# Sample's sums spread over the picking, the first row sums of the second table begun inside it, and the sample's norm moved into it

## The chip, the cores and the metric

The kernel runs on one core of a Trainium2 chip. The metric is device time in microseconds (us), the median over runs; lower is better. The engines are named as in the profile: PE is TensorE (PEld its weight loads), DVE is VectorE, ACT is ScalarE, POOL is GpSimd, SP is SyncE, whose queue issues the plain DMAs; POOL issues the indirect ones (gathers).

## The reference, cut to what matters

One layer of a decoder step: a projection, an RWKV group and a sparse-attention group, an output projection, a norm, and then the part that is changed here, an expert mixer ("PEER") with its norm:

```python
D_MODEL = 2048; SEQ = 256            # prompt tokens
DEC_BATCH, DEC_SEQ = 8, 4            # 32 sample tokens
P_HEADS = 8; P_TOPK = 16; N_EXPERTS = 128 * 128
def peer_ffn(x, wq, subkeys, u_tab, v_tab):
    ...            # per token: 8 heads x 16 = 128 experts, with gates
    h = gelu(einsum('cd,chkd->chk', xb, u_tab[eb]))
    return einsum('chk,chkd->cd', gb * h, v_tab[eb])
f = peer_ffn(x, ...)
x = layer_norm(DEEPNORM_ALPHA * x + f, ln2_g, ln2_b)
```

So each token has 128 gated experts, each a row of 2048 columns in a first table u (for h) and in a second table v (for the sum).

## The kernel before, in words

The mixer is done in two ways at once. For the 256 prompt tokens most columns go the dense way: TensorE multiplies whole rows of the tables, and each token's experts are picked out of the result. The remaining columns go by gathers: for one of a token's 128 experts, POOL issues an indirect DMA that brings 128 rows, one for each token of a half of the prompt (128 partitions x 896 columns of the first table, 128 x 640 of the second), and VectorE makes a dot product of them (the first table, a column of `HD`) or adds them, times their gate, to a running sum (the second table, `fP`). The 32 sample tokens have gathers only: 32 sums `j`, each over four experts of each token at once, where two gathers bring two half rows of v (128 x 1024) and four matmuls with the weights `ws` add them to one bank `fs` of PSUM.

The stages that matter here come in this order:

- The dense loop over the first table (L1886), with prompt gathers of u beside it. Of 256 gathers and dots per partition, 64 are left when it ends (`left`).
- The picking (`M_("weigh")`, L1970 on): 68 steps `s_` of a loop written out in Python, four prompt tokens each. For step u of 64: a one-hot `oo` on VectorE (L1918), its transposes on TensorE (L1922) and their copy `oT` on ScalarE (L1924), products `px` on TensorE (L1930), four masked sums into `E` on VectorE (L1941), the gelu on ScalarE (L1945), the gate into `TB` on VectorE (L1949, `gated`), the one-hot scaled by it on ScalarE or VectorE (L1955, L1957), and `put`: four matmuls `pa` (L1963) and a copy into `AW` (L1964). The stages of u run in steps u to u + 4. Steps 0 to 27 also hold the 64 left dots (L1803). Steps 28 to 59 fetch the sample's sums, steps 30 to 61 add them (L1982). At step 46 the sample's residual and norm weights are loaded, at step 50 the first 128 rows of v (`rows_load(0)`).
- After the loop: both gate tables are transposed into `GE`, the sample's sum gets its residual and its norm (L2027, `norm_quarters`), and sixteen DMAs write it out (L2031).
- The loop over the second table (`M_('V')`, L2085): 128 blocks `k` of 128 rows x 1408 columns. For each block ScalarE makes the high half `vh` (L2077) and VectorE the low half `vl` (L2078) of the loaded `v_`, TensorE does 18 matmuls; for every other block ScalarE makes `ah` (L2074) and VectorE `al` (L2075) from `AW`. Beside it run the 256 prompt gathers of v (`rq`, eight buffers) and their row sums on VectorE (L2058).
- `fin`: the prompt's norm and output.

The order: instructions of the picking that `pin` wraps keep the order in which the code is written, on their engine. The others are placed by a scheduler, which sorts by estimated ready times; ScalarE's casts in the loop over the second table are such. The gathers into the five buffers `rows` of 128 x 1024 (`NRW` = 5, a ring: the dots of the first table and the sample's fetches use the same five) are issued by POOL in order, and each waits for the last reader of the buffer that it fills.

Of the kernel before, what the change touches and what calls it, by code (L numbers as in the profile page):

```python
# [42 lines left out]
NRQ = 8  # L43
# [109 lines left out]
def hybrid_decode_step(ctx: ExitStack, tc: tile.TileContext, a, outs, dbg=None):  # L153
# [19 lines left out]
    def banks(**tags):  # L173

        fewer_banks(0)
        more_banks(**tags)
# [152 lines left out]
    row = 0  # L329
# [126 lines left out]
    def gather(dst, rows_, ix):  # L456
        gp.indirect_dma_start(out=dst, out_offset=None, in_=rows_, in_offset=bass.IndirectOffsetOnAxis(ap=ix, axis=0))  # L457
# [986 lines left out]
    def norm_quarters(pool, x_, g_, b_, tag):  # L1444

        st, mv, rr, sq_ = pool([P, 6], "sst"), pool([P, 2], "smv"), pool([P, 1], "srr"), pool([P, 1], "ssq")
        ve.bn_stats(out=st, in_=x_)
        ve.bn_aggr(out=mv, in_=st)
        ve.tensor_tensor(sq_, mv[:, 0:1], mv[:, 0:1], OP.mult)
        ve.tensor_tensor(mv[:, 1:2], mv[:, 1:2], sq_, OP.add)  # L1450
        pb = bank(tag)
        pe.matmul(pb[:, :2], C0("avg4"), mv, start=True, stop=True)
        ve.tensor_copy(mv, pb[:, :2])
        ve.tensor_tensor(sq_, mv[:, 0:1], mv[:, 0:1], OP.mult)
        ve.tensor_tensor(mv[:, 1:2], mv[:, 1:2], sq_, OP.subtract)
        norm_row(pool, mv, rr)
        sc.activation(x_, x_, AF.Identity, bias=mv[:, 0:1], scale=rr)
        ve.tensor_tensor(x_, x_, g_, OP.mult)
        ve.tensor_tensor(x_, x_, b_, OP.add)
# [309 lines left out]

    M_("wq")  # L1770
    banks(pj=2, pb=6)
    up = Pool("up", "left")
    HD = [up([P, P], f"hd{t}") for t in range(2)]
    TV = [up([P, 8, 16], f"TV{t}") for t in range(2)]
    up([P, 1024], "rows", bufs=NRW)
    xa_ = up([P, 2 * UG], "x1a")
    X1a = [xa_[:, UG * t:UG * t + UG] for t in range(2)]
# [19 lines left out]
    def dot(n=1, upto=2 * P, keep=False, ahead=NRW):  # L1797

        for i in range(got[1], min(got[1] + n, upto)):
            t, s_ = dots[i]  # L1800
            fetch(min(i + ahead, upto))
            r_, h_ = rows_.pop(i), HD[t][:, s_:s_ + 1]
            i_ = ve.scalar_tensor_tensor(r_, r_, 1.0, X1a[t], op0=OP.mult, op1=OP.mult, accum_out=h_)  # L1803
            if keep:
                tc.keep_in_program_order(i_)
            got[1] = i + 1

    def table(t):

        pb = bank("pb")  # L1810
        for q, (op_, v_) in enumerate(((OP.logical_shift_right, 7), (OP.bitwise_and, 127))):
            ii = up([P, P], "ii", I32)
            iff = ii.bitcast(F32)
            ve.tensor_scalar(ii, GI[t], v_, None, op0=op_)
            ve.tensor_copy(iff, ii)
            pe.transpose(pb[:, 128 * q:128 * q + 128], iff, ident)
        pe.transpose(pb[:, 256:384], GE[t], ident)
        pe.transpose(pb[:, 384:], HD[t], ident)
        sc.copy(TB[:, :, P * t:P * t + P], pb.rearrange("p (a b) -> p a b", a=4))
# [151 lines left out]
    ve.tensor_tensor(ws, C0("sum4")[:, None, :32].to_broadcast([P, 32, 32]), GE[2][:, :, None].to_broadcast([P, 32, 32]), OP.mult)  # L1971
    fs, sr = bank("fs"), {}

    def smp_fetch(j):

        for q in range(2):
            sr[j, q] = up([P, 1024], "rows", bufs=NRW)
            gather(sr[j, q], vh2, ig[q][:, j:j + 1])

    def smp_add(j):  # L1980
        for c in range(4):
            pin(pe.matmul(fs[32 * c:32 * c + 32, :], ws[:, j, :], sr[j, c // 2][:, 512 * (c % 2):512 * (c % 2) + 512],  # L1982
                          start=(j == 0), stop=(j == 31)))
# [5 lines left out]
        raw[k] = (vp if k % 3 else vr)([P, FD], "v_", bufs=2 if k % 3 else 1)  # L1989
        return sy.dma_start(raw[k], vtab[P * k:P * k + P, :FD])  # L1990

    left = 2 * P - got[1]
    for s_ in range(68):
        if s_ == 30:
            table(1)
        oT = pick(s_) if s_ < 64 else None
        if 3 <= s_ < 66 and s_ % 2:
            gated(s_ // 2 - 1)
        if s_ >= 4:
            put(s_ - 4)  # L2000
        if 0 <= s_ - 3 < 64:
            scaled(s_ - 3)
        if oT is not None:
            picked(s_, oT)
        if 0 <= s_ - 1 < 64:
            product_of(s_ - 1)
        if s_ < 28:
            dot(-(-left * (s_ + 1) // 28) + 2 * P - left - got[1], keep=True)
        elif s_ < 60:
            smp_fetch(s_ - 28)  # L2010
        if 30 <= s_ < 62:
            smp_add(s_ - 30)
        if s_ == 46:
            bs_, gs_, x_ = (xa_[:, 512 * n:512 * n + 512] for n in range(3))
            for q in range(4):
                r_, c_ = slice(32 * q, 32 * q + 32), slice(512 * q, 512 * q + 512)
                sy.dma_start(x_[r_, :], X1D[NPR:NT, c_])
                for t_, nm in ((gs_, "ln2_g"), (bs_, "ln2_b")):
                    sy.dma_start(t_[r_, :], bass.AP(tensor=a[nm].tensor, offset=a[nm].offset + 512 * q, ap=[[0, 32], [1, 512]]))
        if s_ == 50:  # L2020
            rows_load(0)
    pb = bank("pb")
    for t in range(2):
        pe.transpose(pb[:, 128 * t:128 * t + 128], TB[:, 2, P * t:P * t + P], ident)
        sc.copy(GE[t], pb[:, 128 * t:128 * t + 128])

    ve.scalar_tensor_tensor(x_, x_, ALPHA, fs, op0=OP.mult, op1=OP.add)  # L2027
    norm_quarters(x4p, x_, gs_, bs_, "pb")
    for q in range(4):
        for i in range(4):  # L2030
            sy.dma_start(outs[1][:, i, 512 * q:512 * q + 512], x_[32 * q + 8 * i:32 * q + 8 * i + 8, :])  # L2031
    x4p.close()
    up.close()
    banks(pj=2, pb=6)
# [1 line left out]
    vp = Pool("vp", "left")  # L2036
    vp([P, FD], "v_", bufs=2)
    vp([P, FD], "vh", F32R, bufs=2)
    fP = [vp([P, VG], f"fP{t}") for t in range(2)]
    vp([P, VG], "rq", bufs=NRQ)  # L2040
    queue = [(t, s_) for t in range(2) for s_ in range(P)]
    ahead, here = 0, {}

    def row_fetch(n):

# [4 lines left out]
            gather(here[ahead], a["peer_v_g"], GI[t][:, s_:s_ + 1])  # L2050
            ahead += 1

    def row_add(i):

        t, s_ = queue[i]
        r_, w_ = here.pop(i), GE[t][:, s_:s_ + 1]
        if s_:
            ve.scalar_tensor_tensor(fP[t], r_, w_, fP[t], op0=OP.mult, op1=OP.add)  # L2058
        else:
            ve.tensor_scalar(fP[t], r_, w_, None, op0=OP.mult)  # L2060


    acc = [bank() for _ in range(6)]
    done = 0
    rows_load(1)
    rows_load(2)
    row_fetch(NRQ)
    for k in range(P):
        v_ = raw.pop(k)
        vh, vl = vp([P, FD], "vh", F32R, bufs=2), vp([P, FD], "vl", F32R, bufs=2)  # L2070
        if k % 2 == 0:
            a2 = [vp([P, NPR, 2], nm, F32R, bufs=2) for nm in ("ah", "al")]
            aw_ = AW[:, k // 64, :, k % 64:k % 64 + 2]
            sc.copy(a2[0], aw_)  # L2074
            ve.tensor_tensor(a2[1], aw_, a2[0].bitcast(F32), OP.subtract)  # L2075
        ah, al = (t_[:, :, k % 2] for t_ in a2)
        sc.copy(vh, v_)  # L2077
        lo_ = ve.tensor_tensor(vl, v_, vh.bitcast(F32), OP.subtract)  # L2078
        if k + 3 < P:
            ld_ = rows_load(k + 3)  # L2080
        for t in range(2):
            for wi, xi in ((ah, vh), (ah, vl), (al, vh)):
                for q in range(3):
                    n_ = min(512, FD - 512 * q)
                    pe.matmul(acc[3 * t + q][:, :n_], wi[:, P * t:P * t + P], xi[:, 512 * q:512 * q + n_],  # L2085
                              start=(k == 0 and wi is ah and xi is vh), stop=(k == P - 1 and wi is al))
        while done < min(len(queue), len(queue) * (k + 1) // (P - 2)):
            with tc.issue_after(lo_.ins):
                row_add(done)
            done += 1  # L2090
            row_fetch(done + NRQ)
        if k == 63:
            g2_, b2_, *xo = (AW[:, 0, 32 * n:32 * n + 32, :].rearrange("p a b -> p (a b)") for n in range(4))
        if 66 <= k < 114 and k % 6 == 0:
            with tc.issue_after(ld_.ins):
                n_ = (k - 66) // 6
                c_ = slice(1024 * (n_ % 2), 1024 * (n_ % 2) + 1024)
                if n_ < 4:
# [72 lines left out]
```

## Time and profile before

| | us |
|---|---|
| median of 3 runs (lowest, highest) | 2499.38 (2495.72, 2507.77) |
| the profiled execution, and its span | 2498.71, 2496.9 |
| TensorE busy in the span | 2246.1 (90%) |
| VectorE busy | 1851.9 (74%) |
| ScalarE busy | 927.4 (37%) |
| POOL busy | 1373.4 (55%) |

The span is the time from the first instruction to the last in the profiled execution. A row such as `PE pb L2085` names engine, tile written and source line; a tile's name is followed by the tiles that it was made from (`out<-in`). In rows of groups stand busy time, mean ns of one, and then the engine's idle time just before them and what ended it. "PEclk" is the clock that TensorE was granted, 1.00 being full speed. A wait is written `engine tile line <- releaser: us, times, mean`.

### The profile page before, as it was taken

To read this page: it belongs to the slowest core of one execution; us is meant where nothing else is said; L and a number is where in the kernel's file an instruction comes from. 1 tells how busy PE (TensorE), PEld (TensorE's weight loads), DVE (VectorE), ACT (ScalarE), POOL (GpSimd) and SP (SyncE) were. 2 spreads that over 40 slices of the span, in tenths; PEclk is the share of its full clock that TensorE was granted. 3 is DMA by queue.
4 is the path that set the end of the run, shared out by engine and by line. 5 is a ranking of instruction groups with operands and counts; after the bars stand their busy time and mean duration, and the time that the engine had idled before them with its cause. 6 is when DMAs were issued, how large, how long until landed. Compare 5 with 4: busy or idle time off the path is not lost.

```text
span 2496.9 us, 44823 instructions
## 1 busy us (share of the span) xinstructions
PE 2246.1 (90%) x16396; PEld 1888.6 (76%) x16396; DVE 1851.9 (74%) x4241; ACT 927.4 (37%) x1848; POOL 1373.4 (55%) x1422
## 2 busy tenths in 40 slices
PE   7979999988889997789699999996699799999996
PEld 7967898875545665678598889986676688888785
DVE  5789756554563446889977776779976799988888
ACT  4433222213441333220233343434566444443433
POOL 5677423242444005478655555556656488876662
PEclk9999999998896896899899999997899899999998
DMA  7777975457668884797499999996678599999995
GB/s 219 234 235 232 272 220 172 122 178 223 214 206 269 283 299 148 282 325 241 144 385 372 370 361 357 353 336 221 216 249 294 221 369 356 362 365 361 350 358 186
DMA packets 327613, 684.23 MB, mean 274 GB/s; under 512 B 82270, under 2 KB 200992, under 8 KB 326464
## 3 DMA queue, kind: packets, MB, share of 16 engines
q1 hardware_dynamic: 246176, 342.58, 41.4%
q0 software_dynamic: 81216, 338.78, 38.4%
q8 instruction: 129, 2.11, 0.3%
q14 instruction: 92, 0.75, 0.1%
HBM read 665.69 MB, written 23.88 MB: 276 GB/s over the span
## 4 chain that ended last, share of the span: by engine, by line
PE 60%; DVE 17%; DMA 8%; issue 7%; ACT 4%; POOL 3%; SPq 1%; DVEq 0%; POOLq 0%; ACTq 0%
PE pb L2085 17%; PE ph L1886 10%; PE pj L426 8%; PE ph L1879 3%; PE pa L1668 3%; PE p L1083 2%; DVE rows L1803 2%; DMA co<-in_cache_cmp_kv,gidx 2%; DVE sr L1559 2%; PE pa L1963 2%; DVE ul L1640 2%; PE ss L1500 1%; PE px L1930 1%; PE fs L1982 1%; DVE oo L1918 1%
## 5 line engine op out<-in xcount | busy, mean ns | idle before, releaser
L457 POOL DMA_INDIRECT rows<-in_peer_u_g,gi x256 | 332.3, 1298 | 239.5 <-DVE rows L1803 195.2
L457 POOL DMA_INDIRECT rq<-in_peer_v_g,gi x256 | 378.6, 1479 | 141.8 <-DVE fP L2058 80.2
L1803 DVE SCALAR_TENSOR_TENSOR rows<-rows,x1a 128x896 f32<-128x896 f32 x256 | 272.0, 1092 | 2.9 <-DMA rows<-in_peer_u_g,gi 2.7
L1886 PE MATMUL ph<-XHd,ul 128*128 128x256 f32 x768 | 225.3, 294 | 27.6 <-DVE ul L1640 22.7
L426 PE MATMUL pj<-XH,wl 128*128 128x288 f32 (+1 forms) x752 | 230.1, 306 | 15.2 <-DVE wl L421 9.1
L426 PE MATMUL pj<-XH,wh 128*128 128x288 f32 (+1 forms) x752 | 228.2, 304 | 13.6 <-DVE ss L756 6.9
L1886 PE MATMUL ph<-XHd,uh 128*128 128x256 f32 x768 | 236.7, 308 | 0.0
L2058 DVE SCALAR_TENSOR_TENSOR fP<-rq,ge,fP 128x640 f32<-128x640 f32 x254 | 223.8, 881 | 5.9 <-DMA rq<-in_peer_v_g,gi 3.4
L426 PE MATMUL pj<-XL,wh 128*128 128x288 f32 (+1 forms) x752 | 224.5, 299 | 0.0
L1640 DVE TENSOR_TENSOR ul<-ur,uh 128x384 fp32r<-128x384 f32 x256 | 131.8, 553 | 120.1 <-ACT uh L1639 93.3
L1886 PE MATMUL ph<-XLd,uh 128*128 128x256 f32 x768 | 217.4, 283 | 0.0
L2085 PE MATMUL pb<-vl,ah 128*128 128x512 f32 (+1 forms) x768 | 207.8, 378 | 1.4 <-issue 0.5
L2085 PE MATMUL pb<-vh,ah 128*128 128x512 f32 (+1 forms) x768 | 188.0, 380 | 20.9 <-ACT vh L2077 20.9
L2085 PE MATMUL pb<-vh,al 128*128 128x512 f32 (+1 forms) x768 | 205.7, 376 | 0.0
L419 ACT CAST wh<-wraw 128x512 fp32r<-128x512 f32 (+1 forms) x188 | 114.7, 617 | 223.7 <-PE pj L426 169.0
L1879 PE MATMUL ph<-Xfd,ur 128*128 128x256 f32 x768 | 187.6, 380 | 1.1 <-DMA ur<-in_peer_u_t 1.1
L1886 PEld LDWEIGHTS ph<-XHd,ul 128*128 128x128 f32 x768 | 147.0, 192 | 42.1 <-DVE ul L1640 41.8
L2085 PEld LDWEIGHTS pb<-vh,ah 128*128 128x128 f32 x768 | 145.5, 196 | 43.8 <-ACT vh L2077 24.5
L480 DVE SCALAR_TENSOR_TENSOR CA<-co,wbc,CA 128x256 f32<-128x256 f32 x248 | 133.9, 577 | 45.5 <-DMA co<-in_cache_cmp_kv,gidx 45.2
L2085 PEld LDWEIGHTS pb<-vl,ah 128*128 128x128 f32 x768 | 145.2, 195 | 24.5 <-DVE vl L2078 4.5
L426 PEld LDWEIGHTS pj<-XH,wl 128*128 128x128 f32 (+1 forms) x752 | 142.6, 190 | 26.6 <-DVE wl L421 12.7
L1888 ACT COPY AW<-ph 128x256 f32<-128x256 f32 x128 | 77.8, 608 | 228.1 <-PE ph L1886 198.7
(854 smaller groups left out, 5472.6 us busy)
## 6 DMA issues: line engine op xcount, KB each, us to landing
ur<-in_peer_u_t SPq DMA_DIRECT2D x128, 576.0 KB
wraw<-in_w_in SPq DMA_DIRECT2D x152, 256.0 KB
cw<-in_w_out SPq DMA_DIRECT2D x32, 512.0 KB
wraw<-in_w_out SPq DMA_DIRECT2D x32, 512.0 KB
wraw<-in_peer_wq SPq DMA_DIRECT2D x32, 512.0 KB
cw<-in_peer_wq SPq DMA_DIRECT2D x32, 512.0 KB
wraw<-in_w_in SPq DMA_DIRECT2D x64, 128.0 KB
co<-in_state_win_kv SPq DMA_DIRECT2D x16, 512.0 KB
```

Of the source, the lines that this page charges most:

```text
L419: sc.copy(wh[:, :, :n], w[:, :, :n])
L426: last[2] = pe.matmul(pb[:n, :nt], wi[:, k, :n], xi[(o + k) // 8][:, (o + k) % 8, :nt], start=(o + k == 0 and wi is wh and xi is xh), stop ...
L457: gp.indirect_dma_start(out=dst, out_offset=None, in_=rows_, in_offset=bass.IndirectOffsetOnAxis(ap=ix, axis=0))
L480: ve.scalar_tensor_tensor(d_, x_, w_, d_, op0=OP.mult, op1=OP.add)
L1640: return ve.tensor_tensor(xl, pb, xh.bitcast(F32), OP.subtract)
L1668: pe.matmul(acc[t], xi[:, e, P * t:P * t + P], wi[:, e, :], start=(k == e == n_ == 0), stop=(k == 6 and e == 1 and n_ == 2))
L1803: i_ = ve.scalar_tensor_tensor(r_, r_, 1.0, X1a[t], op0=OP.mult, op1=OP.mult, accum_out=h_)
L1879: pe.matmul(ph[:, :NPR], w[:, e, :], Xfd[:, e - NSP, :], start=(e == NSP), stop=False)
L1886: mm = pe.matmul(ph[:, :NPR], wi[:, e - e0, :], xi[:, e, :], start=False, stop=(e == NSP - 1 and wi is wl))
L1888: return lo_, mm, sc.copy(AW[:, i1 // 64, :, i1 % 64], ph[:, :NPR])
L2058: ve.scalar_tensor_tensor(fP[t], r_, w_, fP[t], op0=OP.mult, op1=OP.add)
L2085: pe.matmul(acc[3 * t + q][:, :n_], wi[:, P * t:P * t + P], xi[:, 512 * q:512 * q + n_], start=(k == 0 and wi is ah and xi is vh), stop=(k ...
```

## The change

It has four parts.

- The sample's 32 sums stand in steps 8 to 57 in place of 30 to 61: eight of them among the dots (steps 10, 12, 15, 17, 20, 22, 25, 27), 24 in four of every five of steps 29 to 57.
- Twenty row sums of the second table (`NRS` = 20, for the first prompt half) stand in steps 39 to 65 of the picking, on VectorE. For them the first gate table is transposed at step 36 (it needs only the tokens of the first half), and the running sum is a tile `fP0` that lies where `HD`, `TV` and `ii` lay, in a pool of its own.
- One list `items` of all fetches of the picking (dots, sample, rows), in the order in which they are used, goes through the ring of five buffers; before the n-th use the first n + 5 have been issued.
- The sample's residual, norm and output are issued at the end of step 59, and not after the loop.

The loop over the second table then does 236 row sums in place of 256. The core of the diff:

```diff
+NRS = 20
...
+    first_sum = fr([P, VG], "fP0")
...
-    def smp_fetch(j):
-
-        for q in range(2):
-            sr[j, q] = up([P, 1024], "rows", bufs=NRW)
-            gather(sr[j, q], vh2, ig[q][:, j:j + 1])
+    def fetch_items(upto):
+
+        for n in range(taken[0], min(upto, len(items))):
+            kind, i, q = items[n]
+            t_ = up([P, 1024], "rows", bufs=NRW)
+            if kind == "dot":
+                rows_[i] = t_[:, :UG]
+                gather(rows_[i], a["peer_u_g"], GI[dots[i][0]][:, dots[i][1]:dots[i][1] + 1])
+            elif kind == "smp":
+                sr[i, q] = t_
+                gather(t_, vh2, ig[q][:, i:i + 1])
+            else:
+                here[i] = t_[:, :VG]
+                gather(here[i], a["peer_v_g"], GI[0][:, i:i + 1])
+        taken[0] = max(taken[0], min(upto, len(items)))
...
+    plan = []
+    for s_ in range(68):
+        n_ = [-(-left * min(x_, 28) // 28) for x_ in (s_, s_ + 1)]
+        plan.append([("dot", 2 * P - left + i, 0) for i in range(*n_)])
+        n_ = [8 * (x_ - 8) // 20 if x_ < 28 else min(32, 8 + 24 * (x_ - 28) // 30) for x_ in (s_, s_ + 1)]
+        plan[-1] += [("smp", j, q) for j in range(max(n_[0], 0), n_[1]) for q in range(2)]
+        n_ = [min(max(NRS * (x_ - 38) // 28, 0), NRS) for x_ in (s_, s_ + 1)]
+        plan[-1] += [("row", i, 0) for i in range(*n_)]
+    items, taken, used = [x_ for st in plan for x_ in st], [got[0] - got[1]], 0
+    def sample_out():
+
+        ve.scalar_tensor_tensor(x_, x_, ALPHA, fs, op0=OP.mult, op1=OP.add)
+        norm_quarters(x4p, x_, gs_, bs_, "pb")
+        for q in range(4):
+            for i in range(4):
+                sy.dma_start(outs[1][:, i, 512 * q:512 * q + 512], x_[32 * q + 8 * i:32 * q + 8 * i + 8, :])
+
+    def row_add(i):
+
+        t, s_ = queue[i]
+        r_, w_ = here.pop(i), GE[t][:, s_:s_ + 1]
+        if s_:
+            return ve.scalar_tensor_tensor(fP[t], r_, w_, fP[t], op0=OP.mult, op1=OP.add)
+        return ve.tensor_scalar(fP[t], r_, w_, None, op0=OP.mult)
+
+    queue = [(t, s_) for t in range(2) for s_ in range(P)]
+    fP = [first_sum]
     for s_ in range(68):
...
-        if s_ < 28:
-            dot(-(-left * (s_ + 1) // 28) + 2 * P - left - got[1], keep=True)
-        elif s_ < 60:
-            smp_fetch(s_ - 28)
-        if 30 <= s_ < 62:
-            smp_add(s_ - 30)
+        if s_ == 36 and NRS:
+            pb = bank("pb")
+            pin(pe.transpose(pb[:, :P], TB[:, 2, :P], ident))
+            pin(sc.copy(GE[0], pb[:, :P]))
+        for kind, i, q in plan[s_]:
+            fetch_items(used + NRW)
+            used += 1
+            if kind == "dot":
+                r_, h_ = rows_.pop(i), HD[1][:, dots[i][1]:dots[i][1] + 1]
+                pin(ve.scalar_tensor_tensor(r_, r_, 1.0, X1a[1], op0=OP.mult, op1=OP.mult, accum_out=h_))
+            elif kind == "row":
+                pin(row_add(i))
+            elif q:
+                smp_add(i)
+        if s_ == 59:
+            sample_out()
...
     pb = bank("pb")
-    for t in range(2):
+    for t in range(1 if NRS else 0, 2):
         pe.transpose(pb[:, 128 * t:128 * t + 128], TB[:, 2, P * t:P * t + P], ident)
         sc.copy(GE[t], pb[:, 128 * t:128 * t + 128])
-
-    ve.scalar_tensor_tensor(x_, x_, ALPHA, fs, op0=OP.mult, op1=OP.add)
-    norm_quarters(x4p, x_, gs_, bs_, "pb")
-    for q in range(4):
-        for i in range(4):
-            sy.dma_start(outs[1][:, i, 512 * q:512 * q + 512], x_[32 * q + 8 * i:32 * q + 8 * i + 8, :])
...
-    ahead, here = 0, {}
+    ahead = NRS
...
-    done = 0
+    done = NRS
     rows_load(1)
     rows_load(2)
-    row_fetch(NRQ)
+    row_fetch(NRS + NRQ)
...
-        while done < min(len(queue), len(queue) * (k + 1) // (P - 2)):
+        while done < min(len(queue), NRS + (len(queue) - NRS) * (k + 1) // (P - 2)):
```

Three places show the new order, on one engine each. On POOL, the fetches of the picking before: the last dots of the first half of the prompt (`gi_70` holds their row numbers), those of the second half (`gi_71`), and then the sample's (`in_peer_v` by `gi_72` and `ig`, two to a sum).

```order
L457 DMA rows<-in_peer_u_g,gi_70 128x896 x122
L457 DMA rows<-in_peer_u_g,gi_71 128x896 x128
L457 DMA rows<-in_peer_v,gi_72 128x1024
L457 DMA rows<-in_peer_v,ig 128x1024
L457 DMA rows<-in_peer_v,gi_72 128x1024
```

And after, from the same place: pairs of the sample stand among the last 37 dots.

```order
L458 DMA rows<-in_peer_u_g,gi_70 128x896 x122
L458 DMA rows<-in_peer_u_g,gi_71 128x896 x91
L458 DMA rows<-in_peer_v,gi_72 128x1024
L458 DMA rows<-in_peer_v,ig 128x1024
L458 DMA rows<-in_peer_u_g,gi_71 128x896 x4
L458 DMA rows<-in_peer_v,gi_72 128x1024
L458 DMA rows<-in_peer_v,ig 128x1024
L458 DMA rows<-in_peer_u_g,gi_71 128x896 x7
L458 DMA rows<-in_peer_v,gi_72 128x1024
L458 DMA rows<-in_peer_v,ig 128x1024
```

What moved is eight pairs, with four or seven dots between them. Further down in the new order, in the second half of the picking, a gather of the second table (`in_peer_v_g`) stands behind most pairs:

```order
L458 DMA rows<-in_peer_v_g,gi_70 128x640
L458 DMA rows<-in_peer_v,gi_72 128x1024
L458 DMA rows<-in_peer_v,ig 128x1024
L458 DMA rows<-in_peer_v_g,gi_70 128x640
L458 DMA rows<-in_peer_v,gi_72 128x1024
L458 DMA rows<-in_peer_v,ig 128x1024
L458 DMA rows<-in_peer_v,gi_72 128x1024
L458 DMA rows<-in_peer_v,ig 128x1024
```

These gathers go into the same five `rows`; before, the first one of the second table came after the last pair, into a ring of its own, `rq`.

On VectorE, the end of the sample's norm before (`srr`, `ln_t`, `smv` are columns of 128 x 1, `x1a` the tile of the sample) and what follows it:

```order
L247 TENSOR_TENSOR ln_t<-srr 128x1
L248 SCALAR_TENSOR_TENSOR ln_t<-ln_t,smv 128x1
L249 SCALAR_TENSOR_TENSOR srr<-ln_t,srr 128x1
L1442 SCALAR_TENSOR_TENSOR smv<-smv,srr 128x1
L1458 TENSOR_TENSOR x1a<-x1a 128x512
L1459 TENSOR_TENSOR x1a<-x1a 128x512
L2075 TENSOR_TENSOR al<-AW,ah 128x512
L2078 TENSOR_TENSOR vl<-v__20256,vh 128x1408
L2075 TENSOR_TENSOR al<-AW,ah 128x512
L2078 TENSOR_TENSOR vl<-v__20899,vh 128x1408
```

And after:

```order
L250 SCALAR_TENSOR_TENSOR srr<-ln_t,srr 128x1
L1443 SCALAR_TENSOR_TENSOR smv<-smv,srr 128x1
L1459 TENSOR_TENSOR x1a<-x1a 128x512
L1460 TENSOR_TENSOR x1a<-x1a 128x512
L1921 TENSOR_TENSOR oo<-CT_61,TB 128x1024
L1944 SCALAR_TENSOR_TENSOR xj,E<-px,oo 128x128 x4
L1947 TENSOR_TENSOR E<-E,TB 128x8
L2029 SCALAR_TENSOR_TENSOR fP_12150<-rows,ge_73,fP_12150 128x640
L1921 TENSOR_TENSOR oo<-CT_61,TB 128x1024
L1952 TENSOR_TENSOR TB<-E,TB 128x8
L1944 SCALAR_TENSOR_TENSOR xj,E<-px,oo 128x128 x4
L2029 SCALAR_TENSOR_TENSOR fP_12150<-rows,ge_73,fP_12150 128x640
```

The norm's last additions stood directly ahead of the loop over the second table (`al`, `vl`); now a one-hot `oo` of step 60 of the picking follows them, with that step's products and one row sum.

On ScalarE, casts in the middle of the loop over the second table, before. The numbers of `v_` rise by one load each:

```order
L2074 CAST ah<-AW 128x512
L2077 CAST vh<-v__22914 128x1408
L2077 CAST vh<-v__22947 128x1408
L2074 CAST ah<-AW 128x512
L2077 CAST vh<-v__22981 128x1408
L2077 CAST vh<-v__23011 128x1408
L2074 CAST ah<-AW 128x512
L2077 CAST vh<-v__23045 128x1408
L2074 CAST ah<-AW 128x512
L2077 CAST vh<-v__23076 128x1408
L2077 CAST vh<-v__23110 128x1408
L2077 CAST vh<-v__23140 128x1408
```

And after, about the same blocks:

```order
L2108 CAST ah<-AW 128x512
L2111 CAST vh<-v__22943 128x1408
L2111 CAST vh<-v__22973 128x1408
L2108 CAST ah<-AW 128x512
L2111 CAST vh<-v__23004 128x1408
L2111 CAST vh<-v__23034 128x1408
L2108 CAST ah<-AW 128x512
L2111 CAST vh<-v__23068 128x1408
L2111 CAST vh<-v__23099 128x1408
```

The regular order is one `ah` and then the two `vh` that are used with it. Before, between `v__23045` and `v__23076`, an `ah` stands between the two `vh` of a pair, and three `vh` follow. Such a place occurs eight times in the loop before and three times after.

More of the change, by code (lines that the diff above doesn't have):

```diff
@@ L1771, in hybrid_decode_step @@
     banks(pj=2, pb=6)
+    fr = Pool("fr", "left")
+    first_sum = fr([P, VG], "fP0")
+    HD = [first_sum[:, P * t:P * t + P] for t in range(2)]
+    TV = [first_sum[:, 2 * P + P * t:3 * P + P * t].rearrange("p (h k) -> p h k", h=8) for t in range(2)]
     up = Pool("up", "left")
-    HD = [up([P, P], f"hd{t}") for t in range(2)]
-    TV = [up([P, 8, 16], f"TV{t}") for t in range(2)]
     up([P, 1024], "rows", bufs=NRW)
@@ L1811, in table @@
         for q, (op_, v_) in enumerate(((OP.logical_shift_right, 7), (OP.bitwise_and, 127))):
-            ii = up([P, P], "ii", I32)
+            ii = first_sum[:, 4 * P:].bitcast(I32)
             iff = ii.bitcast(F32)
@@ L1990, in rows_load @@
         return sy.dma_start(raw[k], vtab[P * k:P * k + P, :FD])
-    left = 2 * P - got[1]
+    left, here = 2 * P - got[1], {}
+    plan = []
[21 more added lines that the diff above has]
+    fP = [first_sum]
     for s_ in range(68):
@@ L2038, in hybrid_decode_step @@
     vp([P, FD], "vh", F32R, bufs=2)
-    fP = [vp([P, VG], f"fP{t}") for t in range(2)]
+    fP.append(vp([P, VG], "fP1"))
     vp([P, VG], "rq", bufs=NRQ)
-    queue = [(t, s_) for t in range(2) for s_ in range(P)]
-    ahead, here = 0, {}
+    ahead = NRS
     def row_fetch(n):
@@ L2051, in row_fetch @@
             ahead += 1
[L2053 to L2060, printed above, removed]
     acc = [bank() for _ in range(6)]
-    done = 0
+    done = NRS
     rows_load(1)
     rows_load(2)
-    row_fetch(NRQ)
+    row_fetch(NRS + NRQ)
     for k in range(P):
@@ L2136, in hybrid_decode_step @@
     vp.close()
+    fr.close()
     gb.close()
```

## The prediction

> **What bounds the kernel now.** I read the page first, for span and chain, then a table of stretches of the second half, then timelines and waits inside the stretches that the diff touches. On the page the chain has no owner outside TensorE, and its largest line is the loop over the second table:
>
> ```profile
> span 2496.9 us, 44823 instructions
> PE pb L2085 17%; PE ph L1886 10%; PE pj L426 8%; PE ph L1879 3%; PE pa L1668 3%; PE p L1083 2%; DVE rows L1803 2%; DMA co<-in_cache_cmp_kv,gidx 2%; DVE sr L1559 2%; PE pa L1963 2%; DVE ul L1640 2%; PE ss L1500 1%; PE px L1930 1%; PE fs L1982 1%; DVE oo L1918 1%
> ```
>
> The order of instructions ahead of the picking is the same before and after, so only what follows 1682 us counts. Cut at the starts of the picking's steps 0, 28, 38, 58, 63, at the loop's first matmul and at its second row of the table:
>
> ```profile
> core 0: us, PE busy (x) PEld busy (x) DVE busy (x) ACT busy (x) POOL busy (x), PEclk, DMA share, GB/s
> 1682.25:1815.62 133.37, 90.29 (x533) 83.19 (x531) 128.28 (x398) 61.49 (x166) 82.01 (x62) 0.78 0.70 219
> 1849.06:1922.04 72.98, 71.98 (x563) 50.40 (x561) 49.12 (x201) 47.90 (x131) 45.85 (x40) 1.00 0.85 290
> 1922.04:1940.33 18.29, 18.29 (x148) 13.18 (x147) 13.46 (x55) 12.34 (x34) 7.31 (x6) 1.00 0.66 227
> 1955.08:1967.30 12.22, 6.65 (x18) 5.31 (x19) 2.36 (x4) 1.91 (x2) 3.60 (x4) 0.64 0.52 155
> ```
>
> Steps 0 to 27 are VectorE's (128.28 of 133.37, 4.76 us a step). Steps 38 to 57 are TensorE's (71.98 of 72.98). The last row is the head of the loop: TensorE works 6.65 us of 12.22, at a granted clock of 0.64.
>
> **Eight sums moved into steps 8 to 27.** A sum costs TensorE about 1 us, and there TensorE has 43 us idle, so its own cost there is nothing; the cover is the dots on VectorE. What it adds is 16 fetches through a ring of five buffers. The fetches of that half, and what they wait for:
>
> ```profile
> L457 POOL DMA_INDIRECT rows<-in_peer_u_g,gi x58 | 77.9, 1343 | 47.6 <-DVE rows L1803 39.4 <-issue 6.4 <-DVE xj L1941 1.8
> q0 software_dynamic: 5028, 28.20, 67.8%
> 1744.06 1.56 POOL L457 DMA_INDIRECT rows<-in_peer_u_g,gi  x1 [1.74 <-DVE rows L1803]
> 1745.50:1746.00 0.50, 0.00 (x0) 0.00 (x0) 0.50 (x3) 0.04 (x1) 0.20 (x2) 0.85 0.04 14
> 1746.00:1748.00 2.00, 1.92 (x17) 1.92 (x18) 1.90 (x10) 0.95 (x2) 0.88 (x1) 1.00 0.74 233
> 1748.00:1750.00 2.00, 0.60 (x6) 0.41 (x4) 2.00 (x5) 1.40 (x5) 1.49 (x1) 1.00 0.71 216
> ```
>
> POOL waits 39.4 us for a dot to free a buffer. Twelve more fetches (58 and 4 stand in that window already) of 1.34 and 0.3 us are 20 us, so POOL still has room. The DMA queue carried 62 fetches in 67.8% of 132 us, 1.44 us each. Steps 8 to 27 will hold 46 dots and 16 sample fetches, 62 x 1.44 = 89 us of 20 x 4.76 = 95: full, but not over. A pair of fetches, the first issued at 1744.06, moves from 1746.0 to 1750.2, so the first lands about 4.1 us after its issue. After a sum, the dot after next step's first finds its buffer freed one step earlier (4.5 us), so most waits are nothing and a third dot in a step is late by about 0.7. I take +3 us: three such dots and small change. The bounds are 0 (POOL's wait absorbs all) and +26 (rival below).
>
> **Steps 28 to 57.** Steps 28 to 37 have eight sums before and after; one more transpose and copy for the gates, +0.5. Steps 38 to 57 lose four sums of twenty and get twelve row sums on VectorE in steps that also have a sum.
>
> ```profile
> 1926.96 1.07 PE L1982 MATMUL fs<-rows,ws 128*32 128x512 f32 x8
> 1929.26 1.22 DVE L1918 TENSOR_TENSOR oo<-CT,TB 128x1024 f32<-128x1024 f32 x1
> 1930.43 1.07 PE L1982 MATMUL fs<-rows,ws 128*32 128x512 f32 x8
> 1931.96 1.22 DVE L1918 TENSOR_TENSOR oo<-CT,TB 128x1024 f32<-128x1024 f32 x1
> POOL rows L457 <- PE fs L1982: 18.8, 19, 2.1
> DVE TB L1949 <- ACT E L1945: 17.0, 9, 2.4
> L2058 DVE SCALAR_TENSOR_TENSOR fP<-rq,ge,fP 128x640 f32<-128x640 f32 x254 | 223.8, 881 | 5.9 <-DMA rq<-in_peer_v_g,gi 3.4
> ```
>
> A step with a sum is 3.47 us (1926.96 to 1930.43); without one I take 2.7, the 2.46 us of VectorE a step (49.12 / 20) and its gaps. Four fewer sums: 4 x 0.77 = -3.1. A row sum is 0.88 us; VectorE idles 17.0 us in these steps waiting for E, so twelve of them (10.6 us) fit. But a row's fetch now stands in POOL's line behind the sample's, and those wait for the sum two steps back (18.8 us of such waits). By the buffers that the built program assigns, six rows (at 42, 46, 47, 51, 56, 57) are issued some 1.3 us or more after such a sum, or behind two sample fetches, and land 4.5 to 5.5 us after the release. VectorE runs about 1 us ahead of what TensorE needs, so each delays TensorE by 0.6 to 0.7: +3.9. Plus 1 for a DMA share of 0.85 that rises. Together +2, bounds -4 (no row is late) and +10 (every one of twelve by the same 0.7 and the fetch).
>
> **Steps 58 to 62, with the norm inside.** The sample's norm is a chain of small instructions on VectorE:
>
> ```profile
> 1949.33 0.16 DVE L1453 COPY smv<-pb 128x2 f32<-128x2 f32 x1 [1.78 <-PE pb L1452]
> 1953.99 0.69 DVE L1459 TENSOR_TENSOR x1a<-x1a 128x512 f32<-128x512 f32 x1
> 1938.51 0.69 DVE L2027 SCALAR_TENSOR_TENSOR x1a<-x1a,fs 128x512 f32<-128x512 f32 x1 [0.39 <-PE fs L1982]
> 1939.32 0.69 DVE L1447 BATCH_NORM_STATS2 sst<-x1a 128x6 f32<-128x512 f32 x1
> ```
>
> From the copy to the last addition are 5.3 us, and in the new order the whole block stands ahead of one oo. Behind that oo wait the transpose, ScalarE's copy and every later step, so its cost is full: it is no longer beside the loop's tail. Five steps: 5 x 2.56 (2.46 and gaps) + 3 row sums x 0.8 + 1.5 (the two 0.69 and the short ones) + 0.7 (wait for the small matmul; 1.78 before) + 5.3 = 22.7; TensorE idles over 5 us there and, as at the loop's head, restarts slowly, +1.4. So 24.1 against 18.29: +6 (bounds 4 and 8).
>
> **The head of the loop.** What stands between the last put and the second row of the table:
>
> ```profile
> 1950.89 0.59 ACT L1964 COPY AW<-pa 128x512 f32<-128x512 f32 x1 [0.73 <-PE pa L1963]
> 1953.67 1.36 ACT L2077 CAST vh<-v__20256 128x1408 fp32r<-128x1408 f32 x1
> 1954.71 6.01 SPq L2031 DMA_DIRECT2D out<-x1a  x16
> 1961.09 0.37 SPq L1990 DMA_DIRECT2D v__20899<-in_peer_v  x1
> 1965.88 1.36 ACT L2077 CAST vh<-v__20899 128x1408 fp32r<-128x1408 f32 x1 [10.26 <-DMA v__20899<-in_peer_v]
> 1967.30 2.72 PE L2085 MATMUL pb<-vh,ah 128*128 128x512 f32 x6 [5.57 <-ACT vh L2077]
> 1981.35 1.44 PE L2085 MATMUL pb<-vh,ah 128*128 128x512 f32 x6
> ```
>
> ScalarE now casts straight after the last put (1951.48 + 1.36 + 0.6), so the first matmul comes at about 1953.4 and not 1955.08: -1.7. SP has issued the sixteen outputs long before, so the second load leaves when the last row sum frees its buffer, near 1948, and its 4.8 us (1961.09 to 1965.88) end before TensorE is through the first row (6.65 us): the hole of 5.6 goes. The second slow start goes too: 2.72 against 1.44 for six matmuls, and half that again behind it, 1.7. Sum -9; bounds -4 (the load leaves late) and -10. Late next are the first three row sums, whose fetches wait for the same buffers.
>
> **The loop over the second table.** It has 20 of 256 fetches fewer, and TensorE waits in it like this:
>
> ```profile
> PE pb L2085 <- ACT vh L2077: 11.1, 8, 1.6
> 2163.50:2186.54 23.04, 23.04 (x110) 20.34 (x109) 21.38 (x21) 10.17 (x9) 19.38 (x13) 1.00 0.98 365
> 2238.71:2263.78 25.07, 23.60 (x109) 20.20 (x109) 23.16 (x25) 11.50 (x10) 16.88 (x12) 1.00 0.99 372
> 2263.78:2288.82 25.04, 23.58 (x109) 20.22 (x109) 21.79 (x23) 9.96 (x9) 15.29 (x12) 1.00 0.96 355
> 2303.30 1.37 ACT L2077 CAST vh<-v__23627 128x1408 fp32r<-128x1408 f32 x1
> 2310.24 0.65 ACT L2074 CAST ah<-AW 128x512 fp32r<-128x512 f32 x1 [5.57 <-PE pb L2085]
> 2310.80 1.36 ACT L2077 CAST vh<-v__23658 128x1408 fp32r<-128x1408 f32 x1
> ```
>
> Six rows take 23.04 us, TensorE's bound; eight times they take 25.05. In each of the eight, ScalarE has the next pair's ah ahead of a vh that is due; ah waits 5.57 us for TensorE's use of its buffer, and vh behind it comes late. That is an order, not a transfer. In the new order this happens three times: five times 2.0, -10. The DMA is near its end too: such a period moves 355 x 25.04 = 8.9 MB, and 0.95 fetch of 0.33 MB fewer, 8.6. In 23.04 us that is 373 GB/s; the best period shows 372. At 355 it would be 24.2 us and the gain 5 x 0.85 = 4. Between -4 and -10 I take -8, as the rows of 365 and 372 lie nearest. [...]
>
> **Sum:** 3 + 0.5 + 2 + 6 - 9 - 8 = -5.5. The profiled execution took 2498.71 us, 0.7 under the median of the three (2499.38), so 2493.
>
> **Rivals.** Faster: no row is late, no dot is late, the norm costs 4 and the loop gains its 10: 0 + 0.5 - 4 + 4 - 9 - 10 = -18.5, 2480. For it speaks the idle time of POOL and VectorE in both halves; against it, the one line of fetches.
> Slower: the fetches become the bound of the dotted half. The pair above moved in 4.2 us, 2.1 each; 46 x 2.1 and 16 x 1.5 (0.85 x 72.98 / 40) are 121 us, against 95: +26 for +3, 2516. It decides once a dot's fetch needs over 1.55 us behind others ((95 - 24) / 46); the queue's mean is 1.44, but its share of 0.7 had gaps in it.
> DMA holds the loop: its eight periods stay at 25 us although the order lets go, -8 becomes 0, 2501.
> The change does not do what it says: the second load leaves no sooner, since its buffer is freed by the last row sums: -9 becomes -4, 2498.
>
> **How the numbers follow.** Forecast 0.5, faster 0.2, slower 0.1, DMA 0.12, late load 0.08. Half a per cent is 12.5 us, about what a measurement can tell here. Faster by more: nine tenths of the second case and a fifth of the forecast's own spread (+-8), 0.28. Slower by more: most of the third, 0.09. The rest is 0.63. The range from 2481 to 2510 takes in the first rival's edge and leaves out the full slow one.
>
> **What would show it.** Dots with a wait for their own fetch: a few us, not twenty. Steps 38 to 57 in 75 us, 58 to 62 in 24 with one VectorE block of 5 us. No second hole at the loop's head. Three waits of TensorE for vh in place of eight. Wrong it would be if dots wait in every step, or if periods without the misplaced ah still take 25 us.

## The result, and the profile after

The changed kernel is slower: 2525.1 us median against 2503.57 us of the kernel before in the same comparison, a ratio of 1.0081 (95% interval 1.0054 to 1.0109). The forecast was 2493 us, inside a range of 2481 to 2510. The page of the profile after:

```profile
span 2525.6 us, 44806 instructions
PE pb L2119 17%; PE ph L1889 7%; POOL rows L458 3%; PE ph L1882 2%; DMA rows<-in_peer_v_g,gi 2%; DVE sr L1560 2%; DMA rows<-in_peer_u_g,gi 2%; DVE ul L1641 1%; PE pa L1966 1%; DVE oo L1921 1%; ACT uh L1640 1%; PE pt L1925 1%; PE px L1933 1%; DVE rows L1413 1%; PE fs L1996 1%
```

In the chain, POOL's gathers into `rows` and the landings of both kinds of prompt rows stand high; before, no gather of this stage was among its largest lines. The spans differ by 28.7 us, but 14.0 of that lies ahead of the picking's step 0 (1682.25 us before, 1696.30 after), where both programs have the same instructions with the same waits. Step 8, which began at 1720.32 us before and at 1734.51 after, came anywhere from 1705.21 to 1729.74 in seven of the runs below, and there that went with the chip and not with the kernel: 1726.16 and 1729.74 in two runs on one chip, 1717.21 to 1723.53 in three on another, 1705.21 and 1709.28 in two on a third. (On which chips the two profiles here were taken is not on record.) So stages are compared from here on, not spans. Steps 8 to 27, 38 to 57, 58 to 62 and the loop's first row, that is its block `k` = 0, after (time, busy time of the engines, granted clock, DMA share, GB/s):

```profile
1734.51:1839.12 104.61, 72.99 (x451) 57.22 (x452) 93.17 (x291) 46.61 (x127) 71.03 (x59) 0.87 0.81 263
1873.36:1963.49 90.13, 70.36 (x548) 51.58 (x546) 59.74 (x216) 49.46 (x136) 54.62 (x48) 0.98 0.75 244
1963.49:1986.82 23.33, 14.97 (x93) 14.39 (x94) 19.51 (x78) 10.85 (x28) 6.26 (x4) 0.78 0.28 74
2001.53:2007.67 6.14, 6.14 (x19) 5.23 (x20) 6.07 (x7) 1.77 (x2) 1.26 (x1) 0.61 1.00 376
```

| stage, us | before | after | difference | predicted |
|---|---|---|---|---|
| steps 0 to 27 | 133.4 | 142.8 | +9.4 | +3 |
| steps 28 to 37 | 33.4 | 34.2 | +0.8 | +0.5 |
| steps 38 to 57 | 73.0 | 90.1 | +17.2 | +2 |
| steps 58 to 62 | 18.3 | 23.3 | +5.0 | +6 |
| step 63 and the loop's first row | 27.0 | 20.9 | -6.1 | -9 |
| rest of the loop | 507.2 | 495.5 | -11.7 | -8 |
| sum | | | +14.6 | -5.5 |

The medians differ by 21.5 us and these stages by 14.6, which lies inside the measured interval (13.5 to 27.3 us). The two halves of the picking with fetches hold the whole error. In steps 38 to 57 TensorE, which was busy 71.98 of 72.98 us before, is now idle for 20. The waits there, after:

```profile
DVE fP L2029 <- DMA rows<-in_peer_v_g,gi: 22.4, 10, 3.0
POOL rows L458 <- DVE fP L2029: 17.6, 9, 3.9
PE pt L1925 <- DVE TB L1952: 11.3, 7, 2.0
PE pt L1925 <- DVE oo L1921: 6.1, 5, 2.1
DVE TB L1952 <- ACT E L1948: 4.3, 3, 1.7
```

VectorE waits 22.4 us for rows of the second table (ten times, 2.2 us each), and TensorE's transposes `pt` wait for the one-hots behind. VectorE's old wait for `E`, 17.0 us before, shrinks to 4.3: the rows took its place and more. The second line closes a circle: POOL in its turn waits for row sums. One turn of it in the timeline after:

```profile
1902.43 0.89 DVE L2029 SCALAR_TENSOR_TENSOR fP<-rows,ge,fP 128x640 f32<-128x640 f32 x1 [1.14 <-DMA rows<-in_peer_v_g,gi]
1903.23 1.22 DVE L1921 TENSOR_TENSOR oo<-CT,TB 128x1024 f32<-128x1024 f32 x1
1903.58 1.68 POOL L458 DMA_INDIRECT rows<-in_peer_v,gi  x1 [1.64 <-DVE fP L2029]
1905.57 0.95 POOL L458 DMA_INDIRECT rows<-in_peer_v,ig  x1 [0.31 <-PE pa L1966]
1905.65 1.22 DVE L1921 TENSOR_TENSOR oo<-CT,TB 128x1024 f32<-128x1024 f32 x1
1906.82 0.96 POOL L458 DMA_INDIRECT rows<-in_peer_v_g,gi  x1 [0.30 <-issue]
1911.65 0.89 DVE L2029 SCALAR_TENSOR_TENSOR fP<-rows,ge,fP 128x640 f32<-128x640 f32 x1 [3.00 <-DMA rows<-in_peer_v_g,gi]
```

A row sum ends at 1903.3 and frees its buffer. The sample's next gather had waited 1.64 us for it; the pair goes first on POOL (to 1906.5), then the next row's gather, which lands 4.8 us after its issue began. From the end of one sum to the start of the next are 8.3 us, where fourteen rows in the 73 us of before would come every 5.2. VectorE waits 3.00 us, and the late sum frees its own buffer late.

In the first half the dots wait for their own fetches, which before they did not in these steps:

```profile
DVE rows L2057 <- DMA rows<-in_peer_u_g,gi: 9.0, 10, 2.0
```

The norm, after: from its first large instruction to the end of its last, and the transposes behind it.

```profile
1964.84 0.68 DVE L2018 SCALAR_TENSOR_TENSOR x1a<-x1a,fs 128x512 f32<-128x512 f32 x1
1975.49 0.69 DVE L1460 TENSOR_TENSOR x1a<-x1a 128x512 f32<-128x512 f32 x1
1976.10 1.22 DVE L1921 TENSOR_TENSOR oo<-CT,TB 128x1024 f32<-128x1024 f32 x1
1977.46 1.09 PE L1925 MATMUL pt<-CT,oo 128*128 128x128 f32 x4 [5.67 <-DVE oo L1921]
```

TensorE waits 5.67 us for the one-hot behind the norm. In the loop the hole of 5.57 us at the second row is gone, and of the eight waits of 1.4 us for a late `vh` three are left, and a shorter one of 0.7 (the first two lines are the first matmuls of rows 0 and 1 in the timeline after; the last two are TensorE's waits from the second row on, after and then before):

```profile
2001.53 2.72 PE L2119 MATMUL pb<-vh,ah 128*128 128x512 f32 x6 [3.57 <-ACT ah L2108]
2007.67 1.44 PE L2119 MATMUL pb<-vh,ah 128*128 128x512 f32 x6
PE pb L2119 <- ACT vh L2111: 4.8, 4, 1.4
```
```profile
PE pb L2085 <- ACT vh L2077: 16.7, 9, 5.6
```

### The profile page after: what moved, and what is told of

Read it like the earlier page. It is cut to its first block, busy times and chain, and to the rows that moved or that the text cites. A ratio compares the mean times of both kernels' runs of the same rounds, so it can differ in the third digit from the quotient of the medians.

```text
span 2525.6 us, 44806 instructions
## 1 busy us (share of the span) xinstructions
PE 2256.6 (89%) x16396; PEld 1894.2 (75%) x16396; DVE 1853.6 (73%) x4241; ACT 926.3 (37%) x1848; POOL 1376.3 (54%) x1422
## 4 chain that ended last, share of the span: by engine, by line
PE 30%; DVE 10%; issue 8%; DMA 6%; POOL 4%; ACT 2%; POOLq 0%; DVEq 0%; ACTq 0%; SPq 0%
PE pb L2119 17%; PE ph L1889 7%; POOL rows L458 3%; PE ph L1882 2%; DMA rows<-in_peer_v_g,gi 2%; DVE sr L1560 2%; DMA rows<-in_peer_u_g,gi 2%; DVE ul L1641 1%; PE pa L1966 1%; DVE oo L1921 1%; ACT uh L1640 1%; PE pt L1925 1%; PE px L1933 1%; DVE rows L1413 1%; PE fs L1996 1%
## 5 line engine op out<-in xcount | busy, mean ns | idle before, releaser
L458 POOL DMA_INDIRECT rq<-in_peer_v_g,gi x236 | 361.0, 1530 | 149.4 <-DVE fP L2029 103.4
L1806 DVE SCALAR_TENSOR_TENSOR rows<-rows,x1a 128x896 f32<-128x896 f32 x194 | 207.3, 1094 | 2.3 <-DMA rows<-in_peer_u_g,gi 1.6
L2029 DVE SCALAR_TENSOR_TENSOR fP<-rq,ge,fP 128x640 f32<-128x640 f32 x235 | 206.9, 880 | 1.9
L1891 ACT COPY AW<-ph 128x256 f32<-128x256 f32 x128 | 77.7, 607 | 228.1 <-PE ph L1889 195.9
L2119 PEld LDWEIGHTS pb<-vl,ah 128*128 128x128 f32 x768 | 145.2, 195 | 21.5 <-DVE vl L2112 2.3
```

Source lines behind the costliest of these rows:

```text
L1891: return lo_, mm, sc.copy(AW[:, i1 // 64, :, i1 % 64], ph[:, :NPR])
L2029: return ve.scalar_tensor_tensor(fP[t], r_, w_, fP[t], op0=OP.mult, op1=OP.add)
```

## The experiments

Theory A: the rows are late because of the ring of five and their place behind the sample on POOL. Rivals: the load on VectorE or on the DMA engines (B), the spread sums themselves (C).

**A sixth buffer.**

```diff
-            t_ = up([P, 1024], "rows", bufs=NRW)
+            t_ = up([P, 1024], "rows", bufs=NRW) if n % 6 != 5 else rx([P, 1024], "rows")
...
-            fetch_items(used + NRW)
+            fetch_items(used + NRW + 1)
...
-        if s_ == 50:
-            rows_load(0)
```

> The changed kernel with a sixth buffer in the ring of fetches during the picking (it lies where the first load of the second table lay, so that load now leaves after the picking). Theory A, the ring: a row's fetch leaves only when the use five places earlier is over, and stands behind a pair of the sample on POOL, so a row lands some 8 us after the row two places earlier was added, and VectorE waits for it with all later one-hots behind it. Then steps 38 to 57 fall from 90.1 us to 74 to 79, VectorE's waits for rows from 22.4 us to under 7, and steps 8 to 27 from 104.6 to 95 to 99; the loop over the second table begins 4 to 6 us later; time by 0.998 to 1.004 of before. Theory B, load: VectorE's added sums (11.5 us) or the DMA engines' rate fill the steps; then steps 38 to 57 stay at 87 or more and steps 8 to 27 at 103 or more, and the time is 1.008 or more of before.

Measured: 0.9987 of before (0.9963 to 1.0011). Steps 8 to 27 and 38 to 57, and what waits in each:

```profile
1729.74:1828.98 99.24, 70.38 (x456) 57.04 (x456) 92.83 (x289) 47.76 (x130) 75.65 (x59) 0.88 0.83 273
1861.76:1942.30 80.54, 68.84 (x536) 50.19 (x535) 59.40 (x217) 48.02 (x132) 53.89 (x46) 1.00 0.77 258
DVE fP L2029 <- DMA rows<-in_peer_v_g,gi: 9.8, 3, 3.5
DVE rows L2057 <- DMA rows<-in_peer_u_g,gi: 3.7, 6, 1.1
```

One buffer takes 9.6 us off the second half and 5.4 off the first, with the engines as busy as before (in the second half VectorE 59.40 us where it was 59.74, the DMA engines 0.77 where they were at 0.75); waits for rows go from ten to three. The load that had to move left at 1695.47 us in the changed kernel, ahead of step 0, so its move plays no part in these stretches. B is out as the main cause, but 80.5 is just above what A allowed.

**No rows in the picking** (`NRS = 0`).

> The changed kernel without the twenty row sums in the picking (all 256 stand in the loop over the second table again); sums spread and norm inside as changed. If the rows alone cost the second half (A or B above), steps 38 to 57 fall from 90.1 to 69 to 72 us and steps 8 to 27 stay at 103 to 106; steps 58 to 62 fall to 20 to 22; time 0.995 to 0.999 of before. If it is the spread sums themselves (theory C: fetches out of order with the steps), steps 38 to 57 stay at 80 or more. The loop over the second table takes 500 to 506 us from its first matmul to its last, if the 20 fetches more cost it nothing, and over 510 if its DMAs hold it.

Measured: 0.9975 (0.9949 to 1.0002).

```profile
1726.16:1830.04 103.88, 73.36 (x452) 56.98 (x453) 93.38 (x291) 46.89 (x128) 72.70 (x59) 0.86 0.82 264
1864.81:1930.91 66.10, 65.66 (x531) 49.03 (x529) 48.92 (x203) 47.68 (x131) 36.51 (x30) 1.00 0.77 255
PE pb L2119 <- ACT vh L2111: 10.9, 8, 1.4
```

The spread sums serve the second half well (66.1 us, C is out), and the first half keeps its cost, which so belongs to the sums and not to the rows. The loop takes 511.0 us, over what was expected if its DMAs cost nothing, but not because of DMAs: the last line shows eight waits for `vh` again, as before. In the trace ScalarE has eight `ah` too early, the same places as before, where the changed kernel has three. So what the rows gained in the loop came from the order into which the scheduler sorted the casts, with 20 sums fewer there.

**The norm after the picking** (the call of `sample_out` moved from step 59 to after the loop).

> The changed kernel with the sample's norm and output after the picking, as before. By the prediction's terms the norm inside costs 5 us in steps 58 to 62 and saves the hole of 5.6 us and a slow start at the loop's head: so steps 58 to 62 fall from 23.3 to 18 to 20 us, the first row of the loop takes 12 us again and not 6.1, and the time is within 4 us of the changed kernel, 1.006 to 1.010 of before. If the norm's chain is dearer than its hole, the time falls by over 6 us.

Measured: 1.0097 (1.0062 to 1.0132). Steps 58 to 62, and the loop's second row:

```profile
1959.93:1976.30 16.37, 12.77 (x91) 11.96 (x92) 15.69 (x60) 10.05 (x27) 4.35 (x3) 0.90 0.31 90
2003.52 2.71 PE L2118 MATMUL pb<-vh,ah 128*128 128x512 f32 x6 [5.94 <-ACT vh L2110]
```

The steps fall by 7.0 us, to 16.4 where 18 to 20 were expected, and from step 63 to the loop's end 7.6 come back. Moving the norm is worth nothing either way.

**ScalarE's casts in the order of the code, on the kernel before.**

```diff
-            sc.copy(a2[0], aw_)
+            pin(sc.copy(a2[0], aw_))
...
-        sc.copy(vh, v_)
+        pin(sc.copy(vh, v_))
```

> The kernel before with ScalarE's casts in the loop over the second table kept in the order of the code (ah, vh, vh), and nothing else. Theory O, order: the eight periods of 25.05 us go to 23.04, waits for vh after the loop's first row from 16.7 to under 7 us (the hole of 5.6 stays), the loop falls by 11 to 17 us of 519.5, time 0.993 to 0.996 of before. Rival, DMA holds the loop: periods of 25 us stay, with another releaser, and the time is 0.998 to 1.001.

Measured: 0.9936 (0.9905 to 0.9966). Six rows at a place like those that took 25.05 us, and TensorE's waits from the second row on:

```profile
2300.00:2323.04 23.04, 23.04 (x109) 20.34 (x109) 21.82 (x23) 9.97 (x9) 18.84 (x12) 1.00 0.98 375
PE pb L2085 <- ACT vh L2077: 7.0, 2, 6.7
```

Of the 7.0 us, 6.7 are the hole in front of the second row; the loop falls to 504.7 us. The order was the cause; with the casts in order six rows take 23.04 us at 375 GB/s, so DMA does not hold this loop at the 372 of the slower periods.

**Rows in two buffers of their own**, fetched two rows ahead; the ring of five for dots and sample alone.

```diff
+                pin(row_add(i))
+                if i + 2 < NRS:
+                    own_fetch(i + 2)
```

> The changed kernel with two buffers of their own for the rows of the second table during the picking, fetched two rows ahead; the ring of five holds the dots and the sample alone (the first load of the second table leaves after the picking). With six buffers steps 38 to 57 still took 80.5 us, with 9.8 us of waits for rows; without rows 66.1. Theory A, the fetch alone: VectorE's waits for rows fall under 4 us and these steps take 67 to 72. Theory V, VectorE's own time for fourteen more sums (12.3 us) can't be hidden: they take 76 to 80 although the waits are gone.

Measured: 1.0006 (0.9981 to 1.0031). Steps 38 to 57, the waits there, and the group of the sample's matmuls:

```profile
1855.01:1932.74 77.73, 71.76 (x537) 52.14 (x536) 59.59 (x216) 48.08 (x132) 52.66 (x44) 0.98 0.81 271
POOL rr L458 <- DVE fP L2032: 8.2, 4, 5.5
DVE TB L1952 <- ACT E L1948: 9.0, 7, 3.9
L1993 PE MATMUL fs<-rows,ws 128*32 128x512 f32 x128 | 19.8, 605 | 0.8 <-DMA rows<-in_peer_v,ig 0.8
```

No wait of VectorE for a row is left, and 77.7 us is what theory V gave. Yet VectorE still waits 12.9 us in front of `TB` (9.0 for `E`, 3.9 for `oo`), and POOL stands up to 5.5 us at a row's gather for the sum two rows back, with the sample's fetches queued behind it (`fs` takes 19.8 us; the same matmuls took 17.1 without rows). So it was open whether VectorE's work or POOL's line costs the 11.6.

**Rows without fetches** settles it: the twenty sums read a tile that lies there already.

```diff
+                here[i] = ws[:, :20, :].rearrange("p a b -> p (a b)")
                 pin(row_add(i))
```

> The changed kernel in which the twenty row sums in the picking read a tile that lies in the chip already (the sample's weights), and their twenty gathers are left out, so the prompt's sum lacks those rows; all else as changed, with the ring of five for dots and sample. Without rows steps 38 to 57 took 66.1 us, with rows in buffers of their own 77.7, as changed 90.1. Theory V (VectorE's 12.3 us for fourteen sums are paid in full): 75 to 79 us. Theory F (in buffers of their own the rows still delayed the sample's fetches on POOL, and VectorE had room): 66 to 71 us. In between, each has its share.

Measured: 0.9961 (0.9936 to 0.9986).

```profile
1848.11:1917.96 69.85, 66.66 (x538) 49.94 (x537) 59.37 (x217) 48.32 (x133) 36.72 (x31) 1.00 0.73 241
PE pt L1925 <- DVE oo L1921: 3.1, 4, 0.9
```

VectorE does the same 59.4 us of work, and the steps take 3.8 us more than without rows. V falls, although its number came out in the run before. Of the 24.0 us that rows cost in these steps (66.1 to 90.1), 3.8 are VectorE's and 20.3 the fetches'. Of these, 12.4 went when the rows had buffers of their own (90.1 to 77.7). The other 7.9 are what the fetches cost even then, by the waits above their place in POOL's line; the DMA engines, at 0.81 there and 0.73 here, were not tried apart from it.

**Half the bytes** for the first eight sums, in as many fetches.

```diff
+                if i < 8:
+                    gather(t_[:, :512], vh4, ig[q][:, i:i + 1])
```

> The changed kernel in which the first eight sums of the sample fetch half the bytes (512 columns in place of 1024, in as many fetches, and the matmuls read those twice; the sample's output leaves out the rest). Five buffers took 104.6 us in steps 8 to 27 and six took 99.2, before 95.3. If bytes in the DMA queue make the dots late, steps 8 to 27 fall to 97 to 100; if it is the count of fetches and the ring, they stay at 102 to 105.

Measured: 1.0042 (1.0019 to 1.0065).

```profile
1723.53:1826.58 103.05, 70.91 (x455) 61.16 (x455) 93.50 (x289) 47.29 (x130) 67.40 (x59) 0.83 0.73 230
```

The DMA engines are at 0.73 in place of 0.81, and the 103.1 us lie among the 102.6 to 104.6 that these steps took in the six kernels with this order, five buffers and all bytes. So bytes are not the cause. The number of fetches on five buffers is the larger part, as a sixth brought 99.2; what keeps that 3.9 us above before was not tried.

**Towards a better version** (called the seventh run below). The fourth run's order of the casts, the picking of before, and the sample's outputs behind the loads of rows 1 and 2:

```diff
+        xn = first_sum[:, :512]
+        ve.scalar_tensor_tensor(xn, x_, ALPHA, fs, op0=OP.mult, op1=OP.add)
...
+    rows_load(1)
+    ld_ = rows_load(2)
+    with tc.issue_after(ld_.ins):
...
```

> The kernel before in its order of the picking (no early sums, no rows, norm after the picking), with ScalarE's casts in the order of the code as in the fourth run, and the sample's norm in a tile that outlives the picking, so that its sixteen output DMAs stand behind the second and third loads of the table on SP. Expected: the hole of 5.6 us at the second row goes, the loop takes 496 to 500 us and not 504.7, time 0.989 to 0.992 of before. Rival: the fourth load now waits behind the outputs and makes the hole at row 3; then the loop takes 503 or more and the time is that of the fourth run, 0.9936.

Measured: 0.9893 (0.9868 to 0.9917), 2473.92 us; again beside the last run, with this expectation:

> The seventh run's kernel again, beside the former on the same chip: 0.987 to 0.992 of before; the loop 501 us.

0.9929 (0.9901 to 0.9957). The loop takes 501.2 and 501.1 us, so the rival has its part: the load of row 3 is late, behind the outputs (the first of the two runs):

```profile
1966.89 1.36 ACT L2113 CAST vh<-v__20922 128x1408 fp32r<-128x1408 f32 x1 [5.88 <-DMA v__20922<-in_peer_v]
```

The same order of casts on the changed kernel without rows:

> The changed kernel without rows (as in the second run) and with ScalarE's casts in the order of the code: sums spread and norm inside, at an order of the casts that is as good as in the seventh run. If only the order separates the second run's loop (511.0 us) from the best, the loop takes 495 to 500 us; the picking keeps its 9 us more in steps 8 to 27 and its 6 us fewer in steps 38 to 57. Time 0.990 to 0.993 of before, so no better than the seventh run; if the spread is worth something, under 0.988.

Measured: 0.9921 (0.9896 to 0.9947). The loop takes 495.5 us with all its 256 gathers:

```profile
1946.08:2441.55 495.47, 494.68 (x2304) 434.42 (x2304) 459.22 (x458) 210.38 (x190) 380.26 (x249) 1.00 0.95 357
```

TensorE is busy all but 0.8 us. From step 0 to the end this version takes 796.0 us, the seventh 795.3: spread sums and a norm inside neither gain nor lose once the order of the casts is mended (102.6 us against 94.9 in steps 8 to 27 and 23.9 against 18.1 in 58 to 62, but 66.1 against 72.7 in 38 to 57 and 495.5 against 501.2 in the loop).

The outputs in fours behind the loads of rows 7 to 10:

> The seventh run's kernel with its sixteen outputs of the sample four by four behind the loads of rows 7 to 10 of the table, in place of all of them behind the load of row 2. In the seventh run rows 3 to 5 of the loop took 5.0, 5.8 and 4.6 us and not 3.84, since the load of row 3 stood behind the outputs (4 us in all). If the outputs do no harm in fours, those rows take 3.84, the loop 496.5 to 498.5 us in place of 501.25, time 0.986 to 0.990 of before. If the loads need SP at once, rows 8 to 11 take the 4 us instead.

Measured: 0.9914 (0.9886 to 0.9941), beside 0.9929 of the seventh run's kernel: no difference. The load of row 3 leaves in time, rows 8 to 11 take 3.84 us each, but row 2 takes 7.2:

```profile
1956.67 0.89 DVE L2028 SCALAR_TENSOR_TENSOR fP<-rq,ge,fP 128x640 f32<-128x640 f32 x1 [3.80 <-DMA rq<-in_peer_v_g,gi]
1960.30 1.62 DVE L2110 TENSOR_TENSOR vl<-v__20880,vh 128x1408 fp32r<-128x1408 f32 x1
1961.97 0.93 PE L2122 MATMUL pb<-vl,ah 128*128 128x512 f32 x3 [2.12 <-issue]
```

Row 2's `vl` stands on VectorE behind the second and third row sums, which wait for their gathers. The hole turned into the next wait in line. All three versions beat both kernels; between them nothing can be told.

## Why the prediction was wrong

- **Steps 38 to 57, the step that failed.** Six late rows that delay TensorE by 0.6 to 0.7 each, +3.9, bounded at +10 with all twelve: this was worked out with the step times of before, each row by itself. But a late row frees its buffer late, POOL holds the sample's pair behind it, and the next row is late again. The six named rows were late, and four more (steps 40, 44, 50, 54), by 2.24 us each on average; +17.2 lies outside the bounds. The runs give the terms: four sums of the sample fewer -6.9 (-3.1 was taken), the sums on VectorE +3.8 (nothing was taken, as they were to fit beside its waits; they were fourteen and not twelve, two in steps without a sample's sum), and their fetches +20.3 (+3.9, and 1 for the DMA share). The wrong part was the loop through the buffers, which a bound made of single delays leaves out.
- **Steps 8 to 27.** Late dots were foreseen, their size was off: +9.3 where +3 was taken. Three late dots of 0.7 us were counted; ten dots waited, 9.0 us in all. The rival of +26 had the right half and the wrong limit: it argued from the transfers, and half the bytes moved nothing beyond the scatter, a sixth buffer 5.4 of the 9.3 us.
- **The norm** at +6 and **the loop's head and rest** at -17 together came out as +5.0 and -17.8. The head gave 6.1 of its 9, as the first matmul came no sooner after step 63: in 14.71 us where it was 14.75. Without rows it came in 13.00, the 1.7 less that were forecast, with ScalarE's first casts in the same order, and with the sums but not their fetches in 13.62. So the three rows of steps 63 to 65 used the 1.7 up, and the forecast had no term for them there. The rest gave 11.7, not 8. DMA as the loop's limit, from which 2 us were taken off, is refuted: six rows took 23.04 us at 375 GB/s, and a stretch of 25.05 us of the fourth run moved 402. The 357 over the 495.5 us of the loop without rows and with pinned casts stand beside a TensorE that idles 0.8 us.
- **Why the loop gained** was stated too simply. The normal place of an `ah` in both kernels is one `vh` ahead of its pair, and not directly ahead of the two that it is used with; the bad places are those two ahead, eight before and three after. One `ah` directly ahead of its two `vh` is the order of the pinned runs. That part of the gain, 10 of 11.7 us, came from where the scheduler put the casts, and two pinned lines alone bring 0.9936.

So the sum was off by 20 us: 15.2 in steps 38 to 57 and 6.4 in the first half, with 1.5 the other way in the rest.

## What to carry to other kernels

A ring of buffers between in-order queues is a loop: add up one turn (release, the line on the issuing queue, issue to landing, use) and compare it with the time in which the uses come round; where it is longer, lateness is passed on from one fetch to the next (here ten of fourteen were late), and a bound made of single late fetches is no bound. Before giving work to an engine's idle time, ask what its data costs: here the sums were almost free and their fetches cost five times as much. When a stage's gain comes from the order in which a scheduler put off-path instructions, try to pin that order first.

## What was not expected of the hardware

In steps 28 to 57 after, a gather's issue on POOL took 0.94 to 0.99 us, but 1.61 to 1.92 (fifteen of them) when it started in the first half of a one-hot `oo` of VectorE; each of these ended 0.8 us after the `oo`. Two lie between: one that started 0.74 us into an `oo` took 1.30, and one that started 0.48 us ahead of an `oo` took 1.39. Above, the gather at 1903.58 begins 0.35 us into the `oo` of 1903.23 and takes 1.68. The gather at 1905.57 began 0.08 us ahead of an `oo` and took 0.95. The other way round it was not seen: the fourteen `oo` of these steps that began during a gather took 1.21 to 1.22 us, like the others. What held the gathers up was not shown.
